# Feed-forward: one matmul of 512 columns for the high weights, with the corrections in a half bank of their own that is added at eviction

## The chip, the cores and the metric

The kernel runs on one core of one Trainium2 chip, in one launch. The metric is the device time of one execution in microseconds (us), the median of several runs.

## The reference

The whole network works on 256 tokens with 1024 features each, in float32. It has two blocks. The first has two layers; each has two feed-forwards and between them a mixer (an RWKV-7 time mix in layer 0, a differential attention with shared keys and values in layer 1). The second block has two attentions side by side with gates (sliding window and stick-breaking), and a PEER layer over 16384 experts. What is computed around the change are the four feed-forwards of the first block:

```python
D_MODEL = 1024; D_FF = 2816; SEQ = 256
def rms_norm(x, g, eps=NORM_EPS):
    xf = x.astype(jnp.float32)
    y = xf * lax.rsqrt(jnp.mean(xf * xf, axis=-1, keepdims=True) + eps)
    return (y * g.astype(jnp.float32)).astype(x.dtype)

def swiglu(h, w_in, w_out):
    gate, up = jnp.split(h @ w_in, 2, axis=-1)
    return (jax.nn.silu(gate) * up) @ w_out
...
for l in range(DEPTH):
    x = x + 0.5 * swiglu(rms_norm(x, ffn_norm[l, 0]), ffn_w_in[l, 0], ffn_w_out[l, 0])
    ...
    x = x + 0.5 * swiglu(rms_norm(x, ffn_norm[l, 1]), ffn_w_in[l, 1], ffn_w_out[l, 1])
```

## The kernel before

**Layout and precision.** Activations are kept transposed: 128 features on the partitions, the 256 tokens as columns, eight such chunks for the 1024 features (`self.x`, tile `xT`). A product in high precision is made from two parts of each operand. A weight tile arrives by DMA (`raw`, 128 x 1024 float32, issued by SyncE, three buffers). `wsplit` makes from it the high part `wh` (ScalarE copies it to float32r, line 255) and the low part `wl` (VectorE subtracts, line 258), four buffers of each. An activation tile (`xs`, or `hh` in the feed-forward) has 512 columns per chunk: the high part in columns 0 to 255, the low part in 256 to 511. `mm3` (line 268) then makes three matmuls of 256 columns into the same half bank of PSUM: `wh` with the high part, `wh` with the low part, `wl` with the high part. `lin` (line 273) does so for a list of chunks. Every matmul of the kernel is recorded at line 243, whatever calls it.

**A feed-forward** (`ffn`, line 402). The 2816 inner features are 22 chunks (`NF`), and for each there is a generator `unit(f)`. It loads two weight tiles (gate and up, eight 128 x 128 weights each), makes 2 x 8 x 3 = 48 matmuls into one PSUM bank of 512 columns (gate in one half, up in the other), and evicts: VectorE multiplies the bank by `rstd`, the reciprocal root of the mean square of each token (line 420, tile `gu`), ScalarE takes Silu of the gate half (line 423), VectorE the product with the up half (line 425, `hv`), and ScalarE and VectorE split it into `hh` (lines 306 and 307). Three units are under way at a time. The scaling of x by the norm's gain has been done ahead, so `rstd` is only needed at eviction; unit 0 computes it.

Then come eight output slices `d`. Each has 22 weights of 128 x 128, in tiles of 8, 8 and 6, and makes 66 matmuls of 256 columns into half a bank. `resid` (line 390) adds half of the sum to x (line 391) and calls `hook`, which prepares the next phase for this chunk: ScalarE scales it by the next norm's gain to the high part of `xs` (line 370, 368 where the low part is not needed), VectorE makes the low part (line 371), ScalarE squares x (line 378) and VectorE adds up the squares (`sqa`, line 379). After the last slice the summed squares go through a small matmul (`smp<-base,sqa`, called the statistics here) to `rstd` (lines 333 and 349).

PSUM banks come from rings by tag: tag mm has two, tag wk four, tag sm two. Units of odd number and odd slices take one of tag mm, the others one of tag wk.

**The stages** in the order of the program, with where they lie in the profile: first feed-forward to about 201 us, RWKV to 482, second feed-forward to 672, third feed-forward to 917, differential attention to 1002, fourth feed-forward to 1190, the second block's attentions to 1365, PEER to the end. The third feed-forward has the projections for the shared keys and values between its units (`extra`); these take banks of tag mm and make their head norms with small matmuls of tag sm.

**What sets the order.** Each engine works its instructions in the order in which they stand; that order comes from the scheduler of the tile framework, which moves instructions of an engine by priority within what their data allow. So the text of the program does not give the order by itself. In the second block the biases of the attention scores are made by ScalarE from a table `btab` (line 733 before, 749 after), which SyncE loads by a DMA (line 840).

Of the kernel before, what the change touches and what calls it, by code (L numbers as in the profile page):

```python
# [9 lines left out]
AF = mybir.ActivationFunctionType  # L10
ALU = mybir.AluOpType
# [3 lines left out]
T = 256  # L15
NF = 22
# [109 lines left out]
def stagger(gens, every, width=99):  # L126
    queue, active, t = list(gens), [], 0
    while queue or active:
        if queue and len(active) < width and (t >= every or not active):
            active.append(queue.pop(0))  # L130
            t = 0
        t += 1
        for g in list(active):
            try:
                next(g)
            except StopIteration:
                active.remove(g)
# [36 lines left out]
class Net:  # L174
# [98 lines left out]
    def lin(self, ps, w, xs, ks, first=True, last=True, j0=0):  # L273
        wh, wl = w
        n = len(ks)
        for j, k in enumerate(ks):
            self.mm3(ps, wh[:, j0 + j], wl[:, j0 + j], xs[:, k], first and j == 0, last and j == n - 1)

    def project(self, src, xs, ps=None):
        w = self.wload(src)  # L280
        p = self.mmt()[:, :T] if ps is None else ps
        self.lin(p, w, xs, range(8))
        return p
# [118 lines left out]
    def ffn(self, n, extra=None, then=None):  # L402
        tc, nc, i = self.tc, self.nc, self.i
        xss, acc = self.begin()
        xs = xss[0]
        with tc.tile_pool(name="ff", bufs=1) as fp:
            hh = fp.tile([128, NF, 512], F32R, name="hh")
            box = {}

            def unit(f):  # L410
                ws = [self.wload(i["ffn_in"][n, f, u]) for u in range(2)]
                yield
                p = self.mmt() if f % 2 else self.wkt("mm")
                for u in range(2):
                    self.lin(p[:, u * T:(u + 1) * T], ws[u], xs, range(8))
                yield
                if f == 0:
                    box["r"] = self.rms(acc)
                t = fp.tile([128, 2, T], F32, name="gu", bufs=2)
                nc.vector.tensor_tensor(t, p.rearrange("p (a b) -> p a b", a=2),  # L420
                                        box["r"][:, None, :].to_broadcast([128, 2, T]), op=ALU.mult)
                s = self.tmp("sg")
                nc.scalar.activation(s, t[:, 0], AF.Silu)
                h = self.tmp("hv")
                nc.vector.tensor_tensor(h, s, t[:, 1], op=ALU.mult)  # L425
                self.split(hh[:, f], h)

            gens = [unit(f) for f in range(NF)]
            if extra:
                more = extra(xss[1], box)  # L430
                gens = gens[:2] + [g for k in range(2, NF) for g in ([gens[k]] + more[k - 2:k - 1])]
            stagger(gens, 1, EVERY["ffn"])
            if then:
                self.pre(then)
            for d in range(8):
                p = (self.mmt() if d % 2 else self.wkt("mm"))[:, :T]
                for k0, k1 in ((0, 8), (8, 16), (16, 22)):
                    w = self.wload(i["ffn_out"][n, d][:, k0:k1], k1 - k0)
                    self.lin(p, w, hh, range(k0, k1), k0 == 0, k1 == NF)
                self.resid(d, p, 0.5)  # L440

    def last_proj(self, src, xs, ready, pin=False):
        early = EVERY["early"]
# [924 lines left out]
```

## Time and profile before

| what | value |
|---|---|
| median of the runs | 2212.38 us |
| runs | 2208.43, 2221.66, 2212.38 us |
| profiled execution, its own time | 2211.49 us |
| its span (first to last instruction) | 2209.7 us |
| granted TensorE clock, mean | 0.994 |
| instructions | 40311 |
| bytes moved by DMA | 351.06 MB, 159 GB/s on the mean |

All durations come from the profiled execution. In the rows below PE is TensorE's matmuls, PEld its weight loads (beside the matmuls), DVE is VectorE, ACT ScalarE, POOL GpSimd, SP SyncE; a q behind a name is the queue that issues its DMAs. "128x256" is partitions by elements. What stands in brackets behind an instruction is how long its engine had stood idle and what ended that. An arrow `a<-b,c` reads "a is written from b and c". A matmul's own duration in a group (281 ns, say) holds its way through the array beside the ones ahead of and behind it; from start to start of matmuls in a row it is less, and that is what a stretch divided by its count gives.

### The profile page before, as it was taken

To read this page: it belongs to the slowest core of one execution; us is meant where nothing else is said; L and a number is where in the kernel's file an instruction comes from. 1 tells how busy PE (TensorE), PEld (TensorE's weight loads), DVE (VectorE), ACT (ScalarE), POOL (GpSimd) and SP (SyncE) were. 2 spreads that over 40 slices of the span, in tenths; PEclk is the share of its full clock that TensorE was granted. 3 is DMA by queue.
4 is the path that set the end of the run, shared out by engine and by line. 5 is a ranking of instruction groups with operands and counts; after the bars stand their busy time and mean duration, and the time that the engine had idled before them with its cause. 6 is when DMAs were issued, how large, how long until landed. Compare 5 with 4: busy or idle time off the path is not lost.

```text
span 2209.7 us, 40311 instructions
## 1 busy us (share of the span) xinstructions
PE 2169.1 (98%) x16048; PEld 2032.6 (92%) x16048; DVE 1533.2 (69%) x2982; ACT 1116.3 (51%) x2070; POOL 78.0 (4%) x109
## 2 busy tenths in 40 slices
PE   8999999989999999999999999999999999999999
PEld 8998777779999999989999999999999999888887
DVE  6665695666666666486666767999489985666665
ACT  5443633344454444475445654444576654554554
POOL 0000040000000000020001000000000000000000
PEclk9999999999999999999999999999999999999999
DMA  6564331135565555435565445555544345555554
GB/s 214 183 180 141 117 105 39 39 105 182 180 183 179 167 179 178 136 112 189 183 180 179 136 145 172 163 172 176 192 138 131 130 145 187 192 192 195 194 192 152
DMA packets 98589, 351.06 MB, mean 159 GB/s; under 512 B 10944, under 2 KB 12480, under 8 KB 98272
## 3 DMA queue, kind: packets, MB, share of 16 engines
q1 hardware_dynamic: 98400, 348.48, 49.2%
q8 instruction: 126, 2.06, 0.4%
q14 instruction: 63, 0.52, 0.1%
HBM read 347.38 MB, written 1.05 MB: 158 GB/s over the span
## 4 chain that ended last, share of the span: by engine, by line
PE 48%; DVE 5%; issue 1%; ACT 0%; DMA 0%; POOLq 0%; POOL 0%; ACTq 0%
PE mm L243 28%; PE y L243 16%; PE pg L243 3%; DVE wl L258 2%; DVE dm L1130 1%; DVE ex L1135 0%; PE sc L243 0%; DVE dm L1133 0%; PE po L243 0%; DVE v L1098 0%; PE tr L762 0%; PE psc L243 0%; DMA raw<-in_p_u_dram 0%; DVE si L1100 0%; PE smp L243 0%
## 5 line engine op out<-in xcount | busy, mean ns | idle before, releaser
L243 PE MATMUL mm<-xs,wh 128*128 128x256 f32 x6304 | 1160.4, 286 | 14.0 <-ACT wh L255 6.8
L243 PEld LDWEIGHTS mm<-xs,wh 128*128 128x128 f32 x6304 | 988.3, 193 | 20.4 <-ACT wh L255 6.8
L258 DVE TENSOR_TENSOR wl<-raw,wh 128x1024 fp32r<-128x1024 f32 (+1 forms) x633 | 765.9, 1210 | 328.0 <-ACT wh L255 327.0
L255 ACT ACTIVATE wh<-raw 128x1024 fp32r<-128x1024 f32 (+1 forms) x633 | 660.5, 1044 | 594.7 <-PE mm L243 472.5
L243 PE MATMUL mm<-xs,wl 128*128 128x256 f32 x3152 | 896.6, 285 | 2.0 <-DVE wl L258 2.0
L243 PEld LDWEIGHTS mm<-xs,wl 128*128 128x128 f32 x3152 | 607.2, 193 | 2.9 <-DVE wl L258 2.9
L243 PE MATMUL y<-wh,cs 128*128 128x512 f32 x1024 | 274.0, 390 | 0.0
L243 PE MATMUL mm<-hh,wh 128*128 128x256 f32 x1408 | 250.1, 281 | 0.0
L243 PEld LDWEIGHTS y<-wh,cs 128*128 128x128 f32 x1024 | 192.3, 188 | 39.6
L243 PEld LDWEIGHTS mm<-hh,wh 128*128 128x128 f32 x1408 | 215.9, 188 | 0.0
L243 PE MATMUL mm<-hh,wl 128*128 128x256 f32 x704 | 198.1, 281 | 0.0
L243 PE MATMUL y<-wl,cs 128*128 128x512 f32 x512 | 157.8, 390 | 0.0
L243 PEld LDWEIGHTS mm<-hh,wl 128*128 128x128 f32 x704 | 132.6, 188 | 0.0
L243 PE MATMUL mm<-xs,raw 128*128 128x256 f32 x512 | 126.1, 394 | 2.5 <-DVE xs L490 2.5
L243 PEld LDWEIGHTS y<-wl,cs 128*128 128x128 f32 x512 | 96.2, 188 | 20.0
L306 ACT ACTIVATE cs<-ga 128x256 fp32r<-128x256 f32 x103 | 43.0, 418 | 136.9 <-PE y L243 136.7
L243 PEld LDWEIGHTS mm<-xs,raw 128*128 128x128 f32 x512 | 96.2, 197 | 16.9 <-DVE xs L490 2.9
L420 DVE TENSOR_TENSOR gu<-mm,rstd 128x512 f32<-128x512 f32 x88 | 60.8, 691 | 44.4 <-PE mm L243 44.2
L306 ACT ACTIVATE hh<-hv 128x256 fp32r<-128x256 f32 x88 | 36.6, 416 | 104.6 <-DVE hv L425 104.6
L307 DVE TENSOR_TENSOR cs<-ga,cs 128x256 fp32r<-128x256 f32 x103 | 43.8, 426 | 55.1 <-ACT cs L306 55.1
L1045 DVE TENSOR_SCALAR ohb<-iota,xT 128x128 f32<-128x128 f32 x192 | 59.5, 343 | 15.3 <-PE pg L243 13.9
L243 PE MATMUL pg<-ohb,xT 128*128 128x128 f32 x512 | 65.9, 276 | 0.0
(320 smaller groups left out, 1883.9 us busy)
## 6 DMA issues: line engine op xcount, KB each, us to landing
raw<-in_ffn_in_dram SPq DMA_DIRECT2D x176, 512.0 KB, 3.8
raw<-in_p_u_dram SPq DMA_DIRECT2D x128, 512.0 KB, 3.7
raw<-in_p_v_dram SPq DMA_DIRECT2D x128, 512.0 KB, 4.3
raw<-in_ffn_out_dram SPq DMA_DIRECT2D x64, 512.0 KB, 3.6
raw<-in_w_in_dram SPq DMA_DIRECT2D x34, 512.0 KB, 3.7
raw<-in_ffn_out_dram SPq DMA_DIRECT2D x32, 384.0 KB, 3.3
raw<-in_w_rkv_dram SPq DMA_DIRECT2D x24, 512.0 KB, 3.7
raw<-in_w_kv_dram SPq DMA_DIRECT2D x16, 512.0 KB, 3.7
```

The lines of the kernel that those rows point to most:

```text
L243: self.nc.tensor.matmul(out, lhsT, rhs, start=start, stop=stop, skip_group_check=True)
L255: hi = nc.scalar.activation(fh[:rows, :w], raw[:rows, :w], AF.Copy)
L258: lo = nc.vector.tensor_tensor(fl[:rows, :w], raw[:rows, :w], fh[:rows, :w].bitcast(F32), op=ALU.subtract)
L306: nc.scalar.activation(dst[rows, :T], src, AF.Copy)
L307: nc.vector.tensor_tensor(dst[rows, T:], src, dst[rows, :T].bitcast(F32), op=ALU.subtract)
L420: nc.vector.tensor_tensor(t, p.rearrange("p (a b) -> p a b", a=2), box["r"][:, None, :].to_broadcast([128, 2, T]), op=ALU.mult)
L1045: nc.vector.tensor_scalar(b, iota, itp[:, 1, t:t + 1], itp[:, 2, t:t + 1], op0=ALU.is_equal, op1=ALU.mult)
L1130: nc.vector.tensor_tensor(m, iota[:, None, :50].to_broadcast([128, 16, 50]), bf[:, h, :, None].to_broadcast([128, 16, 50]), op=ALU.is_equal)
```

## The change

A new `linw` makes, for each chunk, one matmul of 512 columns with `wh` (both parts of the activation at once, into the two halves of a bank) and one of 256 columns with `wl` and the high part, into the second half. The first half then holds high times high, the second both corrections. A new `fold` adds the halves at eviction: ScalarE copies the second half out of PSUM (`low`), VectorE adds the first half to it. A unit now takes two banks, one of tag mm for the gate and one of tag wk for the up half, and two folds; only the gate half is multiplied by `rstd` there. The up half stays unscaled, and so does `hh`; in its place every output slice is multiplied by `rstd` after its fold (tile `fy`), before `resid`. The output slices take a whole bank each. The rest of the program keeps `lin`.

```diff
+    def linw(self, ps, w, xs, ks, first=True, last=True):
+        wh, wl = w
+        n = len(ks)
+        for j, k in enumerate(ks):
+            self.mm(ps, wh[:, j], xs[:, k], first and j == 0, False)
+            self.mm(ps[:, T:], wl[:, j], xs[:, k, :T], False, last and j == n - 1)
+
+    def fold(self, out, p):
+        low = self.tmp("low")
+        self.nc.scalar.activation(low, p[:, T:], AF.Copy)
+        self.nc.vector.tensor_tensor(out, p[:, :T], low, op=ALU.add)
...
-                p = self.mmt() if f % 2 else self.wkt("mm")
-                for u in range(2):
-                    self.lin(p[:, u * T:(u + 1) * T], ws[u], xs, range(8))
+                ps = [self.mmt(), self.wkt("mm")]
+                for p, w in zip(ps, ws):
+                    self.linw(p, w, xs, range(8))
                 yield
                 if f == 0:
                     box["r"] = self.rms(acc)
                 t = fp.tile([128, 2, T], F32, name="gu", bufs=2)
-                nc.vector.tensor_tensor(t, p.rearrange("p (a b) -> p a b", a=2),
-                                        box["r"][:, None, :].to_broadcast([128, 2, T]), op=ALU.mult)
+                for u, p in enumerate(ps):
+                    self.fold(t[:, u], p)
+                nc.vector.tensor_tensor(t[:, 0], t[:, 0], box["r"], op=ALU.mult)
...
-                p = (self.mmt() if d % 2 else self.wkt("mm"))[:, :T]
+                p = self.mmt() if d % 2 else self.wkt("mm")
                 for k0, k1 in ((0, 8), (8, 16), (16, 22)):
                     w = self.wload(i["ffn_out"][n, d][:, k0:k1], k1 - k0)
-                    self.lin(p, w, hh, range(k0, k1), k0 == 0, k1 == NF)
-                self.resid(d, p, 0.5)
+                    self.linw(p, w, hh, range(k0, k1), k0 == 0, k1 == NF)
+                y = self.tmp("fy")
+                self.fold(y, p)
+                nc.vector.tensor_tensor(y, y, box["r"], op=ALU.mult)
+                self.resid(d, y, 0.5)
```

The numbers behind the names below tell tiles apart; the two programs count them differently. Lines of the changed program: fold 288 and 289, multiply of the gate 434, product 438, split of `hv` 319, multiply of an output slice 455, residual 403, scaling 382, square 390, sum of squares 391, `rstd` 361.

VectorE in one unit of the first feed-forward (`gu` the gate and up half, `wl` the low weights of later tiles, `hv` the product), before:

```order
L420 TENSOR_TENSOR gu_773<-mm_712,rstd_210 128x512
L258 TENSOR_TENSOR wl_839<-raw_836,wh_838 128x1024
L425 TENSOR_TENSOR hv_777<-sg_775,gu_773 128x256
L307 TENSOR_TENSOR hh_148<-hv_777,hh_148 128x256
L258 TENSOR_TENSOR wl_902<-raw_899,wh_901 128x1024
```

and in the changed program:

```order
L289 TENSOR_TENSOR gu_566<-mm_520,low_567 128x256
L434 TENSOR_TENSOR gu_566<-gu_566,rstd_195 128x256
L258 TENSOR_TENSOR wl_623<-raw_620,wh_622 128x1024
L289 TENSOR_TENSOR gu_566<-mm_521,low_570 128x256
L438 TENSOR_TENSOR hv_576<-sg_574,gu_566 128x256
L258 TENSOR_TENSOR wl_677<-raw_674,wh_676 128x1024
L319 TENSOR_TENSOR hh_148<-hv_576,hh_148 128x256
```

One instruction on 512 columns became three on 256, and the two splits of weights now stand between the additions and between the product and its split.

ScalarE from the end of the fourth feed-forward into the second block (`xs` the scaling of the last chunk of x, `sq` its square, `bias` made from the table `btab`), before:

```order
L255 ACTIVATE wh_13430<-raw_13428 128x1024
L255 ACTIVATE wh_13475<-raw_13473 128x1024
L370 ACTIVATE xs_12685<-xT_64,vec_65 128x256
L378 ACTIVATE sq_13324<-xT_64 128x256
L255 ACTIVATE wh_13521<-raw_13519 128x1024
L349 ACTIVATE rstd_13328<-smp_13329 128x256
L733 ACTIVATE bias_13423<-btab_13342 128x384
L733 ACTIVATE bias_13425<-btab_13342 128x384
```

and in the changed program:

```order
L255 ACTIVATE wh_12094<-raw_12092 128x1024
L255 ACTIVATE wh_12139<-raw_12137 128x1024
L288 ACTIVATE low_11981<-mm_11917 128x256
L749 ACTIVATE bias_12087<-btab_12006 128x384
L749 ACTIVATE bias_12089<-btab_12006 128x384
L382 ACTIVATE xs_11468<-xT_64,vec_65 128x256
L390 ACTIVATE sq_11988<-xT_64 128x256
L749 ACTIVATE bias_12132<-btab_12006 128x384
L749 ACTIVATE bias_12134<-btab_12006 128x384
L255 ACTIVATE wh_12185<-raw_12183 128x1024
L361 ACTIVATE rstd_11992<-smp_11993 128x256
```

Two biases moved ahead of the scaling and the square of the last chunk, and two more ahead of the next weight split and `rstd`.

VectorE at the end of the first feed-forward (`xT` the residual, `sqa` the sum of squares, `sm` the first step of the statistics, `oka` a constant of the RWKV stage), before:

```order
L391 SCALAR_TENSOR_TENSOR xT_64<-mm_2199,xT_64 128x256
L258 TENSOR_TENSOR wl_2479<-raw_2476,wh_2478 128x1024
L379 TENSOR_TENSOR sqa_1752<-sqa_1752,sq_2285 128x256
L391 SCALAR_TENSOR_TENSOR xT_64<-mm_2288,xT_64 128x256
L476 TENSOR_SCALAR oka_2389<-vec_65 128x8
L379 TENSOR_TENSOR sqa_1752<-sqa_1752,sq_2374 128x256
L333 TENSOR_SCALAR sm_2404<-smp_2401 128x2
```

and in the changed program:

```order
L258 TENSOR_TENSOR wl_2145<-raw_2142,wh_2144 128x1024
L391 TENSOR_TENSOR sqa_1537<-sqa_1537,sq_1968 128x256
L492 TENSOR_SCALAR oka_2055<-vec_65 128x8
L289 TENSOR_TENSOR fy_2034<-mm_1971,low_2035 128x256
L455 TENSOR_TENSOR fy_2034<-fy_2034,rstd_195 128x256
L403 SCALAR_TENSOR_TENSOR xT_64<-fy_2034,xT_64 128x256
L391 TENSOR_TENSOR sqa_1537<-sqa_1537,sq_2040 128x256
L345 TENSOR_SCALAR sm_2070<-smp_2067 128x2
```

Ahead of the last residual there now stand the addition and the multiply of its slice; what follows the residual is as before.

## Rows read from the trace of the kernel before

**Rows 1.** The page: busy time of each engine, and the granted clock in 40 slices.
```profile
PE 2169.1 (98%) x16048; PEld 2032.6 (92%) x16048; DVE 1533.2 (69%) x2982; ACT 1116.3 (51%) x2070; POOL 78.0 (4%) x109
...
PEclk9999999999999999999999999999999999999999
```
**Rows 2.** Chain of waits in order of time, last stretch: start us, us, what.
```profile
1813.61 43.20 PE mm L243 x360
1856.80 348.20 PE y L243 x1536
```
**Rows 3.** Busy times by stretch: a unit, an output slice, units of the third feed-forward.
```profile
core 0: us, PE busy (x) PEld busy (x) DVE busy (x) ACT busy (x) POOL busy (x), PEclk, DMA share, GB/s
63.52:69.28 5.76, 5.76 (x50) 5.76 (x49) 3.90 (x6) 2.73 (x5) 0.00 (x0) 1.00 0.56 186
185.39:193.22 7.83, 7.83 (x68) 7.83 (x67) 4.17 (x5) 3.20 (x4) 0.00 (x0) 1.00 0.62 190
672.00:853.00 181.00, 180.48 (x1495) 178.59 (x1495) 115.51 (x169) 83.17 (x122) 9.61 (x9) 1.00 0.53 173
```
**Rows 4.** Timeline of a unit: start us, us, instruction, idle before it.
```profile
63.44 1.06 ACT L255 ACTIVATE wh<-raw 128x1024 fp32r<-128x1024 f32 x1 [1.70 <-PE mm L243]
63.52 0.69 DVE L420 TENSOR_TENSOR gu<-mm,rstd 128x512 f32<-128x512 f32 x1 [0.52 <-PE mm L243]
```
**Rows 5.** Groups by line, shapes apart: count, busy us, mean ns, idle before.
```profile
L243 PE MATMUL mm<-hh,wl 128*128 128x256 f32 x704 | 198.1, 281 | 0.0
...
L258 DVE TENSOR_TENSOR wl<-raw,wh 128x1024 fp32r<-128x1024 f32 x600 | 734.0, 1224 | 288.3 <-ACT wh L255 287.2
...
L255 ACT ACTIVATE wh<-raw 128x1024 fp32r<-128x1024 f32 x600 | 632.4, 1055 | 545.8 <-PE mm L243 430.0 <-issue 63.8 <-DMA raw<-in_p_u_dram 20.6
...
L420 DVE TENSOR_TENSOR gu<-mm,rstd 128x512 f32<-128x512 f32 x88 | 60.8, 691 | 44.4 <-PE mm L243 44.2
...
L425 DVE TENSOR_TENSOR hv<-sg,gu 128x256 f32<-128x256 f32 x88 | 37.0, 421 | 3.4 <-ACT sg L423 3.4
...
L391 DVE SCALAR_TENSOR_TENSOR xT<-mm,xT 128x256 f32<-128x256 f32 x56 | 23.3, 423 | 25.5 <-PE mm L243 25.3
...
L991 ACT ACTIVATE ga<-mm 128x256 f32<-128x256 f32 x60 | 22.0, 367 | 1.7 <-PE mm L243 1.7
```
**Rows 6.** Timeline of the first feed-forward's end, TensorE and VectorE.
```profile
200.74 0.28 PE L243 MATMUL mm<-hh,wl 128*128 128x256 f32 x1
...
201.05 0.42 DVE L391 SCALAR_TENSOR_TENSOR xT<-mm,xT 128x256 f32<-128x256 f32 x1 [4.17 <-PE mm L243]
...
202.44 0.61 PE L243 MATMUL smp<-base,sqa 128*128 128x1 f32 x4 [1.43 <-DVE sqa L379]
```
**Rows 7.** Timeline of the third feed-forward's end, TensorE and VectorE.
```profile
917.41 2.32 PE L243 MATMUL mm<-xs,raw 128*128 128x256 f32 x10
...
917.61 0.42 DVE L391 SCALAR_TENSOR_TENSOR xT<-mm,xT 128x256 f32<-128x256 f32 x1 [6.01 <-PE mm L243]
...
919.57 0.50 PE L243 MATMUL smp<-base,sqa 128*128 128x1 f32 x4
```
**Rows 8.** Timeline of the fourth feed-forward's end, all engines.
```profile
1190.76 0.33 SPq L840 DMA_DIRECT2D btab<-in_t_b_dram  x1
...
1191.62 0.49 ACT L370 ACTIVATE xs<-xT,vec 128x256 fp32r<-128x256 f32 x1
...
1192.88 0.48 DVE L371 SCALAR_TENSOR_TENSOR xs<-xT,vec,xs 128x256 fp32r<-128x256 f32 x1
...
1193.28 0.42 DVE L379 TENSOR_TENSOR sqa<-sqa,sq 128x256 f32<-128x256 f32 x1
...
1193.76 0.60 PE L243 MATMUL smp<-base,sqa 128*128 128x1 f32 x4
...
1196.20 1.75 ACT L733 ACTIVATE bias<-btab 128x384 f32<-128x384 f32 x4
```
**Rows 9.** View of the tile btab: from its DMA's issue to its landing.
```profile
DMA to landing us min/median/max: 5.4/5.4/5.4
```
**Rows 10.** Busy times by stretch behind the first feed-forward, columns as in rows 3.
```profile
204.00:206.00 2.00, 0.69 (x2) 0.29 (x2) 0.78 (x2) 0.38 (x1) 0.03 (x1) 0.50 0.00 0
```

## The prediction

> **What bounds the kernel now.** I read the page's busy times first [rows 1]: TensorE is busy 98% of the span, VectorE 69%, ScalarE 51%, and the row of granted clocks shows full speed in every slice. Then the chain of waits in order of time, whose last pieces are TensorE alone [rows 2]: 360 matmuls of 256 columns take 43.20 us, 120.0 ns each, and 1536 of 512 columns take 348.20 us, 226.7 ns each. So a matmul costs its columns (106.7 and 213.3 ns at 2.4 GHz) plus 13.3 ns, whichever its width. The reader is to see that two narrow ones cost 240.0 ns and one wide one 226.7.
>
> Then the busy times of one unit and of one output slice [rows 3]. A unit (48 matmuls, 5.76 us, 120.0 ns each) and a slice of the output projection (66 matmuls, 7.83 us, 118.6 ns each) are filled by TensorE; VectorE works 3.90 and 4.17 us in them. The timeline of the unit [rows 4] says who waits for whom: ScalarE waits 1.70 us for TensorE to free a weight buffer, VectorE 0.52 us for the sums. So the feed-forward ends with TensorE, and what TensorE loses there is worth its full time.
>
> **The change part by part.** *Fewer matmuls.* Two matmuls of 256 columns with the same high weights become one of 512. Feed-forward has 4 x 22 x 2 x 8 = 1408 such pairs in the input part and 4 x 8 x 22 = 704 in the output part (the 704 low matmuls of [rows 5] count the latter), so 2112 matmuls go; columns stay the same. Input part: 240.0 - 226.7 = 13.3 ns each, 0.213 us a unit, 18.8 us over 88 units. Output part: 2 x 118.6 = 237.3 ns; a wide one there I take at 213.3 + 12.6, between the two overheads that rows show (12.0 and 13.3), so 11.3 ns each, 7.9 us. Together 26.7 us. The bounds from rows: nothing, if a wide matmul took twice 118.6 to 120 ns here, and 28.2 us, if all 2112 saved 13.3.
>
> Of the rules on this, one speaks against the change. The Trainium skill (TensorE: Matmul & The Clock Gate, Back-to-back issue gap) puts a warm matmul at its columns over 2.4 GHz plus 2.5 ns; by it only 2112 x 2.5 = 5.3 us would go, an estimate. The trace does not agree at either width: 120.0 and 226.7 ns stand where the rule has 109 and 216.
>
> *More work at eviction.* Per unit VectorE loses one 512-column multiply (691 ns) and gets two additions and one multiply of 256 columns; the addition reads PSUM and SBUF as the residual does (423 ns), the multiply is like the 421 ns product [rows 5]. That is +0.57 us: 4.5 us in a unit of 5.55. ScalarE gets two copies out of PSUM, like the 367 ns Gelu that reads it: +0.73 us. In an output slice VectorE gets 0.85 us and ScalarE 0.37. I cost this at nothing while the units run: it lies beside TensorE, in ScalarE's 1.70 us of waiting and in VectorE's 1.86 us without work (5.76 - 3.90). The new order of VectorE puts a weight split between the additions, so nothing stands idle behind the second copy. Four weight buffers let the splits run two half units ahead. In PSUM a unit now takes one bank of each kind; the bank of tag mm comes back two units later, and its addition is done half a unit after the sums. In the third feed-forward the key/value projections share that tag, so a bank alternates between a unit and a projection; VectorE works 115.5 of 181 us there now [rows 3] and gets 22 x 0.57 = 12.5 us more. DMA gets 1 MB per 5.55 us, 189 GB/s, beside the 186 of the unit and 190 of the slice [rows 3].
>
> *The end of each feed-forward.* The last slice is now copied, added, multiplied by rstd and only then added to x: one copy (0.37, with its hand-off 0.41) and two VectorE operations of 0.42, so x is 1.25 us later. What that costs differs at the four ends.
> - Into the RWKV stage [rows 6]: last matmul at 200.74, residual 201.05, statistics matmul 202.44 after 1.43 us of idle TensorE. Nothing covers: +1.25 us.
> - Into the second attention [rows 7]: TensorE runs the ready matmuls of the query projection until the statistics start at 919.57, with no gap. All later steps hang on them: +1.25 us.
> - From the second to the third feed-forward: the new order gives TensorE thirteen pairs of the two halves of the first unit, some 4.7 us, before it needs the last chunk of x, which comes about 4.6 us after the last matmul: a weight split stands in the way (1.06 + 1.22), then copy 0.37, three VectorE operations of 0.42, scaling 0.49 and low part 0.48 in part beside it [rows 5, 8]: 0, and up to 1 us if that is short.
> - Into the second block [rows 8]: here a queue is changed. ScalarE's order now has two biases, made from a table that a DMA brings, ahead of the scaling of the last chunk of x; before, they stood behind rstd. That DMA is issued at 1190.76 (it waits for the memory of hh) and lands 5.4 us later [rows 9], at 1196.2. Behind it come two biases (4 take 1.75 us, 0.44 each), the scaling (ready after 0.49), the low part (0.48) and the square sum (0.42): statistics at about 1198.45, against 1193.76 before. The order puts 17 more matmuls (42 for 25) ahead of them, 2.0 us. So +2.7 us. The ends: 0 if the table is early enough, 4.7 if those matmuls do not help.
>
> I add 0.7 us for what I cannot place: in [rows 10] the granted clock is at half after TensorE idled at the first of these ends (1.2 GHz between 204 and 206), a longer idle at the second block may do the same (bounds 0 and 1.5 us), and the third feed-forward has short waits of TensorE for head norms.
>
> Sum, on the profiled execution's own 2211.5 us (span 2209.7 and 1.8 around it; 0.04% below the median of 2212.4): - 18.8 - 7.9 + 1.25 + 1.25 + 2.7 + 0.7 = - 20.8, so 2190.7, rounded to 2191. That is 1.0% below the median: right on the border of what a measurement of this kernel can tell from no change, 1%.
>
> **The rivals.**
> *The ends cost little.* If the table lands before it is needed and the second attention's wait is filled, of the four ends 2.5 us stay: 2211.5 - 26.7 + 2.5 = 2187.3. For it: TensorE has ready matmuls at three of the four ends. Against it: the table's 5.4 us is a row, and its issue waits for the last matmul. 0.15.
>
> *The overhead is not per matmul here.* If what I call overhead went with the columns moved, a wide matmul would take 2 x 120.0 ns here: nothing saved, and 5.9 us of ends added: 2217. For it: no row has wide and narrow matmuls in turn, nor xs or hh as the moving operand of a wide one. Against it: the 226.7 ns of [rows 2] are measured over 1536 wide ones in a row. 0.08. (With the saving by the rule of the Trainium skill above, 5.3 us, this case would be at 2212.)
>
> *ScalarE and VectorE become the bound of the units (slower).* Each unit is now handed over more often: copy, add, multiply, Silu, product, split, all in order with the weight splits. If VectorE keeps the 1.86 us per unit that it stands idle now and works 4.47 (3.90 + 0.57), a unit takes 6.33 us in place of 5.76: 88 x 0.57 = 50 us lost, with 7.9 gained in the output part and 6 lost at the ends, 2260. It decides from 5.78 us a unit on (no gain left) and is slower by over 1% from 6.03. Against it: part of that idle time is waiting for TensorE itself [rows 4], which shrinks when others get slower, and four weight buffers absorb single delays. 0.11.
>
> **How the numbers follow.** The forecast has 0.66, with its own range 2186 to 2196; about 0.37 of these are more than 1% below 2212.4 (under 2190.3), the rest within 1%. Faster by over 1%: 0.25 of the forecast and 0.14 of the early table, 0.39. Same: 0.41 of the forecast, 0.08 of the second rival and 0.01 of the first, 0.50. Slower: 0.11, of which nearly all over 1%. The range goes from 2184 to 2218: it holds the forecast, the early table and no gain, and leaves out the slower rival and the tails.
>
> **What would show it.** Right: a unit of 5.55 us and an output slice of 7.57 to 7.60 between the same points, wide matmuls some 227 ns apart and the next narrow one 120 behind; 2112 fewer matmuls on the page; TensorE as full as now in the units, VectorE near 4.5 us of them. Behind the first feed-forward the statistics 2.6 to 2.7 us after the last matmul in place of 1.7; at the second block ScalarE's bias with a wait for the table's DMA, and TensorE idle for 2 to 3 us ahead of the statistics. Wrong: units of 5.7 us with a full TensorE (the overhead stayed), matmuls that wait for wh, wl or a copy within the units (the others became the bound), or no wait at the second block.

## The result and the profile after

| | median, us | runs | ratio to before, 95% interval |
|---|---|---|---|
| before, beside it | 2214.22 | 5 | |
| changed | 2198.59 (2197.19 to 2203.62) | 5 | 0.994 [0.9928, 0.9952] |
| before, with the next set of runs | 2210.14 | 17 | |
| changed, once more | 2197.40 (2195.70 to 2199.57) | 6 | 0.9941 [0.9927, 0.9954] |

So 0.6% faster, 13 to 16 us, where 21 us were forecast: within the range and within 1%. The profiled execution (2203.62 us, span 2201.8) is the longest of the five. In the RWKV stage TensorE had 0.59 of its clock between 446 and 467 us, and 0.84 there before:

```profile
446.00:467.00 21.00, 15.43 (x67) 12.15 (x67) 9.27 (x25) 4.92 (x10) 2.15 (x2) 0.59 0.00 1
```
```profile
446.00:467.00 21.00, 15.46 (x95) 12.18 (x96) 11.91 (x35) 5.16 (x11) 2.15 (x2) 0.84 0.00 1
```

Whether the change has a part in that is not shown: the same program has 0.67 there in run 1 below, and run 3, which ends its feed-forwards as before, has 0.66. So the stages are compared one by one, and the total of this trace comes at the end.

The page after, busy times and granted clock, answers to [rows 1]:

```profile
PE 2156.8 (98%) x13936; PEld 1927.3 (88%) x13936; DVE 1594.9 (72%) x3222; ACT 1171.6 (53%) x2278; POOL 79.5 (4%) x109
...
PEclk9999999989999999999999999999999999999999
```

The 2112 matmuls are gone (16048 to 13936), and TensorE is as full as before. Busy times by stretch (columns as in [rows 3]) first for one unit and one output slice, then for long stretches of two input parts and two output parts:

```profile
62.23:67.89 5.66, 5.66 (x34) 4.89 (x33) 4.31 (x9) 3.27 (x6) 0.00 (x0) 1.00 0.59 185
182.21:189.92 7.71, 7.71 (x47) 6.75 (x46) 4.93 (x7) 3.55 (x5) 0.00 (x0) 1.00 0.61 195
...
40.00:120.00 80.00, 80.00 (x455) 69.34 (x454) 60.78 (x100) 46.80 (x86) 0.00 (x0) 1.00 0.58 187
1010.00:1110.00 100.00, 100.00 (x579) 88.23 (x578) 77.54 (x127) 58.88 (x108) 0.00 (x0) 1.00 0.58 190
...
140.00:190.00 50.00, 50.00 (x287) 43.85 (x286) 31.63 (x44) 22.25 (x32) 0.00 (x0) 1.00 0.62 192
852.00:902.00 50.00, 50.00 (x290) 43.99 (x289) 31.71 (x47) 25.88 (x39) 0.00 (x0) 1.00 0.64 186
```

A unit went from 5.76 to 5.66 us, not to 5.55; a slice from 7.83 to 7.71, not to 7.60. The long stretches show why. A count has about two matmuls that reach in over the border; without them the first input part gives 80.00/453 = 176.6 ns a matmul, **353 ns for a pair of wide and narrow**, and the fourth, by the same instructions with the same full TensorE and clock, 100.00/577 = 173.3, **347 ns a pair**. The forecast was 226.7 + 120.0 = 346.7. The output parts differ too: 351 ns a pair in the first feed-forward, 347 in the third. There are two paces, where the rows of before had shown only narrow ones at 120.0 and at 118.6 ns.

Groups by line, shapes apart, for the eviction ([rows 5] has what they replace):

```profile
L255 ACT ACTIVATE wh<-raw 128x1024 fp32r<-128x1024 f32 x600 | 633.6, 1056 | 577.2 <-PE mm L243 294.3 <-issue 232.2 <-DMA raw<-in_p_u_dram 18.4
...
L288 ACT ACTIVATE low<-mm 128x256 f32<-128x256 f32 x208 | 75.9, 365 | 16.3 <-PE mm L243 16.3
L289 DVE TENSOR_TENSOR gu<-mm,low 128x256 f32<-128x256 f32 x176 | 73.3, 418 | 0.5 <-ACT low L288 0.5
...
L434 DVE TENSOR_TENSOR gu<-gu,rstd 128x256 f32<-128x256 f32 x88 | 37.4, 425 | 3.6 <-ACT rstd L361 0.8
```

Copy 365 ns, addition 418, multiply 425: the forecast took 367, 423 and 421. VectorE works 4.31 us in a unit, 4.5 were forecast.

The end of the first feed-forward in the timeline answers to [rows 6]:

```profile
197.51 0.28 PE L243 MATMUL mm<-hh,wl 128*128 128x256 f32 x1
...
197.83 0.38 ACT L288 ACTIVATE low<-mm 128x256 f32<-128x256 f32 x1 [5.50 <-PE mm L243]
...
198.25 0.42 DVE L289 TENSOR_TENSOR fy<-mm,low 128x256 f32<-128x256 f32 x1 [0.24 <-ACT low L288]
198.70 0.42 DVE L455 TENSOR_TENSOR fy<-fy,rstd 128x256 f32<-128x256 f32 x1
199.16 0.42 DVE L403 SCALAR_TENSOR_TENSOR xT<-fy,xT 128x256 f32<-128x256 f32 x1
...
200.55 1.01 PE L243 MATMUL smp<-base,sqa 128*128 128x1 f32 x4 [2.76 <-DVE sqa L391]
```

Copy, addition, multiply and residual stand in a row, and the statistics come 3.04 us after the last matmul in place of 1.70: 1.34 more, 1.25 forecast. TensorE idles 2.76 us instead of 1.43, and the granted clock behind that is lower. Twelve microseconds from just ahead of the statistics, before and after:

```profile
202.00:214.00 12.00, 8.07 (x30) 6.45 (x31) 9.32 (x26) 0.38 (x1) 0.70 (x1) 0.72 0.11 27
```
```profile
200.00:212.00 12.00, 7.92 (x24) 6.33 (x25) 8.85 (x25) 0.42 (x2) 0.70 (x1) 0.57 0.01 4
```

The granted clock is 0.57 on the mean, 0.72 before: more of the stretch is spent at 1.2 GHz, the lower of the two levels. Into the second attention (against [rows 7]) the statistics come 3.44 us after the last matmul, 2.27 before:

```profile
910.56 0.28 PE L243 MATMUL mm<-hh,wl 128*128 128x256 f32 x1
...
914.00 0.61 PE L243 MATMUL smp<-base,sqa 128*128 128x1 f32 x4
```

And the end of the fourth feed-forward, to hold against [rows 8] and [rows 9]:

```profile
1180.25 0.33 SPq L856 DMA_DIRECT2D btab<-in_t_b_dram  x1
...
1183.08 0.94 ACT L749 ACTIVATE bias<-btab 128x384 f32<-128x384 f32 x2 [1.61 <-DMA btab<-in_t_b_dram]
...
1185.46 0.50 PE L243 MATMUL smp<-base,sqa 128*128 128x1 f32 x4
...
1187.06 0.43 PE L357 MATMUL smp<-base,sm 128*128 128x128 f32 x2 [0.51 <-POOL sm L348]
...
1188.42 0.39 PE L243 MATMUL mm<-xs,wh 128*128 128x256 f32 x1 [0.69 <-DVE pj L868]
```

ScalarE does wait for the table (1.61 us), as the order said. But the table lands 2.8 us after its issue, not 5.4 as before, and TensorE has matmuls until the statistics (one wait, of 0.16 us). What idles comes behind them (0.51 and 0.69 us), since `rstd` is late.

### The profile page after: what moved, and what is told of

Same layout as the page of the kernel before. It is cut to its first block, busy times and chain, and to the rows that moved or that the text cites. A ratio compares the mean times of both kernels' runs of the same rounds, so it can differ in the third digit from the quotient of the medians.

```text
span 2201.8 us, 36597 instructions
## 1 busy us (share of the span) xinstructions
PE 2156.8 (98%) x13936; PEld 1927.3 (88%) x13936; DVE 1594.9 (72%) x3222; ACT 1171.6 (53%) x2278; POOL 79.5 (4%) x109
## 4 chain that ended last, share of the span: by engine, by line
PE 48%; DVE 5%; issue 1%; ACT 0%; DMA 0%; POOLq 0%; POOL 0%; ACTq 0%
PE mm L243 28%; PE y L243 16%; PE pg L243 3%; DVE wl L258 2%; DVE dm L1146 0%; PE sc L243 0%; DVE ex L1151 0%; DVE dm L1149 0%; PE po L243 0%; DVE v L1114 0%; PE tr L778 0%; PE psc L243 0%; ACT wh L255 0%; DVE si L1116 0%; DMA raw<-in_p_u_dram 0%
## 5 line engine op out<-in xcount | busy, mean ns | idle before, releaser
L243 PE MATMUL mm<-xs,wh 128*128 128x256 f32 (+1 forms) x4896 | 1149.4, 319 | 17.0 <-ACT wh L255 6.9
L243 PEld LDWEIGHTS mm<-xs,wh 128*128 128x128 f32 x4896 | 814.7, 192 | 84.1 <-ACT wh L255 6.9
L243 PE MATMUL mm<-hh,wh 128*128 128x512 f32 x704 | 246.5, 393 | 0.0
L243 PEld LDWEIGHTS mm<-hh,wh 128*128 128x128 f32 x704 | 132.2, 188 | 30.2
L288 ACT ACTIVATE low<-mm 128x256 f32<-128x256 f32 x208 | 75.9, 365 | 16.3 <-PE mm L243 16.3
L289 DVE TENSOR_TENSOR gu<-mm,low 128x256 f32<-128x256 f32 x176 | 73.3, 418 | 0.5 <-ACT low L288 0.5
```

What stands on the lines that cost most here:

```text
L243: self.nc.tensor.matmul(out, lhsT, rhs, start=start, stop=stop, skip_group_check=True)
L288: self.nc.scalar.activation(low, p[:, T:], AF.Copy)
L289: self.nc.vector.tensor_tensor(out, p[:, :T], low, op=ALU.add)
```

## The experiments

Two questions: what sets the pace of a pair, and what the ends cost. All medians stand beside 2210 to 2211 for the kernel before.

**1. The changed kernel again** (nothing edited).

> The changed kernel once more, nothing edited. In the trace after the change a pair of a wide and a narrow matmul takes either 346.7 ns from start to start (all of the second and fourth feed-forward's input parts, 226.7 + 120.0 as predicted) or 351 to 354 ns (the first one's input part, half of the third's, most output parts). Theory A (the pace is fixed by the program, by what lies where): the same stretches show the same pace again, and the median is again 2197 to 2201 us. Theory B (the pace is left over from a chance disturbance ahead): other stretches are slow now, 7 ns x 352 pairs = 2.5 us an input part, and single runs spread by several us.

2197.40 us, in the table above. The same two stretches and the second feed-forward's:

```profile
40.00:120.00 80.00, 80.00 (x464) 70.53 (x463) 62.28 (x101) 47.41 (x87) 0.00 (x0) 1.00 0.59 193
490.00:590.00 100.00, 100.00 (x568) 86.70 (x567) 76.52 (x125) 57.67 (x107) 0.00 (x0) 1.00 0.55 184
1010.00:1110.00 100.00, 100.00 (x578) 88.16 (x578) 77.66 (x127) 58.88 (x108) 0.00 (x0) 1.00 0.59 189
```

The first input part is now at the fast pace (80.00/462 = 173.2, 346 ns a pair), the second at the slow one (353 ns), which it was not in the first trace (100 us held 576 there). One program, two executions, other stretches: theory B for the input parts. The output parts have the same pace in both (x286 and x291 in the stretches shown above, x287 and x290 there).

**2. Wide ones together, narrow ones together.**

```diff
         for j, k in enumerate(ks):
             self.mm(ps, wh[:, j], xs[:, k], first and j == 0, False)
+        for j, k in enumerate(ks):
             self.mm(ps[:, T:], wl[:, j], xs[:, k, :T], False, last and j == n - 1)
```

> The same matmuls, but for each weight tile all wide ones first and then all narrow ones, in place of pairs in turn. Theory A (turn by turn is what costs: a pair in turn can fall into a slower pace): every pair takes 226.7 + 120.0 = 346.7 ns or less, first input part 2.5 us shorter than after the change, output parts 0.8 us each, third input part about 1.5: 6 to 7 us less than the changed kernel, about 2192 us. Rival (the overhead is only half saved because it goes with the data, or with the operands' places): no change against the changed kernel, 2198 us, and pairs of 351 to 354 in the same stretches.

2196.36 us, 0.994 [0.9922, 0.9958]: no change against the changed kernel. The first feed-forward's stretch:

```profile
40.00:120.00 80.00, 80.00 (x458) 70.28 (x458) 61.93 (x101) 46.87 (x87) 0.00 (x0) 1.00 0.59 192
```

80.00/456 = 175.4, some 350 ns for a wide and a narrow one (in groups of eight the stretch need not hold as many of both), between the two paces. Turn by turn is not what costs; theory A falls. The third output part lost the faster pace here (x285 in 852 to 902 us, x290 with the change).

**3 and 4. One part alone.** Input part: the unit as changed, with `rstd` on both halves, and the output loop of before. Output part: the unit of before, and wide output slices with copy and addition.

```diff
-                    self.linw(p, w, hh, range(k0, k1), k0 == 0, k1 == NF)
-                y = self.tmp("fy")
-                self.fold(y, p)
-                nc.vector.tensor_tensor(y, y, box["r"], op=ALU.mult)
-                self.resid(d, y, 0.5)
+                    self.lin(p, w, hh, range(k0, k1), k0 == 0, k1 == NF)
+                self.resid(d, p, 0.5)
```

```diff
-                ps = [self.mmt(), self.wkt("mm")]
-                for p, w in zip(ps, ws):
-                    self.linw(p, w, xs, range(8))
+                p = self.mmt() if f % 2 else self.wkt("mm")
+                for u in range(2):
+                    self.lin(p[:, u * T:(u + 1) * T], ws[u], xs, range(8))
...
                 self.fold(y, p)
-                nc.vector.tensor_tensor(y, y, box["r"], op=ALU.mult)
                 self.resid(d, y, 0.5)
```

> The wide matmuls in the input part alone; the output part is that of the kernel before, one half bank, no copy and no addition, and rstd is multiplied into both halves of the unit again (one VectorE multiply of 512 columns in SBUF, longer than the 256-column one by 0.2 to 0.4 us a unit). By my steps the input part has 12 to 15 us of the gain in the changed kernel's trace and the ends lose nothing here: 2199 to 2202 from 2214. If VectorE sets the pace of the units (rival), slower than the changed kernel by several us.

2196.51 us, 0.9939 [0.9923, 0.9954]. From the first matmul to the first output matmul it took 126.70 us, 131.38 before and 128.90 in the first trace of the change: the first input part was at the fast pace here.

> The wide matmuls in the output part alone, with copy and addition ahead of the residual but no multiply by rstd there (the units are those of the kernel before). By the changed kernel's trace each output part saves 0.9 us, 3.6 in all, and each end is late by a copy and an addition, 0.8 us, at three ends: about 1 us of gain, 2213, not to be told from before. If the output part's saving were the 7.9 us that I predicted: 2209.

2211.20 us, 1.0001 [0.9991, 1.0012]. The input part alone has the whole gain (run 3). The output part gives 0.9 us each time (62.54 to 61.66 from its first to its last matmul) and loses it at the ends.

**5. The last slice as before.** `rstd` goes back into both halves in the units; slices 0 to 6 are wide, slice 7 narrow.

```diff
-                    self.linw(p, w, hh, range(k0, k1), k0 == 0, k1 == NF)
+                    (self.lin if d == 7 else self.linw)(p, w, hh, range(k0, k1), k0 == 0, k1 == NF)
```

> All wide as in the change, but the last output slice of each feed-forward is the narrow one of before (no copy, no addition), and rstd is multiplied into both halves in the units, not into the output slices. Theory (the ends cost what the copy, the addition and the multiply put ahead of the last residual): the statistics come 1.7 and 2.3 us after the last matmul again behind the first and third feed-forward (3.04 and 3.44 with the change), and the output part keeps 7/8 of its 0.88 us: 62.54 - 0.77 = 61.8. With 352 pairs an input part at 7 to 13 ns each the median is 2193 to 2196 us beside 2210. Rival (the end is covered anyway, it is the clock that costs): as the changed kernel, 2197.

2191.53 us, 0.9908 [0.9892, 0.9923]: about 6 us better than the changed kernel, more than forecast. The statistics come 1.71 and 2.27 us after the last matmul again, and the clock behind the first end is back to 0.72:

```profile
197.00:209.00 12.00, 8.11 (x30) 6.53 (x31) 9.32 (x26) 0.38 (x1) 0.70 (x1) 0.72 0.09 28
```

From that end's last matmul to the first output matmul of the second feed-forward it took 403.55 us, against 409.01 in run 1. Of the 5.46 some 2.3 are the pace of the second input part (352 pairs at 346 in place of 353), 1.33 the end itself; the remaining 1.8 go with a higher clock, here and between 446 and 467 us (0.84, and 0.67 in run 1). The pace and that later clock differ between executions without such an edit too, so the trace bears out the ends, and not the whole 6 us.

**6 and 7. The place of the moving operand.** What sets the output parts apart is where hh starts: behind 16 KB of shared keys and values and one small tile in the third feed-forward, 16416 bytes further on. So tiles were moved by 32 bytes in each partition, with a tile of 8 floats ahead of them.

```diff
+            if n != 2:
+                pad = fp.tile([128, 8], F32, name="pad")
+                nc.gpsimd.memset(pad[:, :1], 0.0)
             hh = fp.tile([128, NF, 512], F32R, name="hh")
```

> As the run with the narrow last slice, and hh of the first, second and fourth feed-forward starts 32 bytes further in each partition (a tile of 8 floats ahead of it), so that it starts at a multiple of 64 bytes as it does in the third, behind the shared keys and values. In the traces so far an output pair takes 351.7 ns in the first, second and fourth feed-forward and 346.8 in the third, in every run. Theory A (the place of the moving operand sets that pace): 346 to 347 in all four, 0.8 us less at three output parts, 2.4 us in all. Theory B (it is something else in the third feed-forward, such as its other transfers): no change, 351.7 in the three.

2189.82 us, 0.990 [0.9884, 0.9916]. Stretches of 45 us in the first, second and third output part:

```profile
138.00:183.00 45.00, 45.00 (x261) 39.65 (x260) 27.06 (x36) 20.81 (x31) 0.00 (x0) 1.00 0.62 191
612.00:657.00 45.00, 45.00 (x261) 39.61 (x261) 30.83 (x46) 25.91 (x42) 0.00 (x0) 1.00 0.64 193
850.00:895.00 45.00, 45.00 (x261) 39.66 (x260) 26.62 (x37) 23.57 (x36) 0.00 (x0) 1.00 0.62 187
```

261 in each, and 250 in 43 us of the fourth: 347 ns a pair in all of them. Theory A. (The third had no new pad and is as before.) The median does not tell this run from run 5. Then the xs tiles:

```diff
         self.xp = pool("acts", bufs=1)
+        pad = self.xp.tile([128, 8], F32, name="pad")
+        nc.gpsimd.memset(pad[:, :1], 0.0)
```

> As the run with the narrow last slice, and both xs tiles start 32 bytes further, at a multiple of 64; everything behind them moves along, so hh is at a multiple of 64 in the first, second and fourth feed-forward and 32 bytes over one in the third. Theory A (place of the moving operand): output pairs 346.7 in the first, second and fourth, 351.7 in the third, the other way round than before; and the input part has one pace, 346.7, in all feed-forwards, in place of one of two by chance. Theory B (not the place): 351.7 in the first, second and fourth and 346.8 in the third as ever, and input parts at either pace.

2188.75 us, 0.9898 [0.9882, 0.9914]. Third and fourth output part, and PEER's wide matmuls:

```profile
842.00:885.00 43.00, 43.00 (x246) 37.31 (x245) 24.84 (x33) 21.47 (x33) 0.00 (x0) 1.00 0.62 189
1112.00:1155.00 43.00, 43.00 (x250) 37.85 (x249) 27.38 (x39) 22.14 (x34) 0.00 (x0) 1.00 0.63 190
...
1900.00:2100.00 200.00, 200.00 (x858) 161.01 (x858) 118.11 (x144) 97.81 (x143) 0.00 (x0) 1.00 0.57 188
```

The other way round, as forecast: the third output part is now the slow one (352 ns), and all four input parts hold 347 ns (three of the four did in run 5 too). The median does not tell this run from runs 5 and 6. But PEER lost: 200 us hold 858 wide matmuls there, 233 ns each, and 884 before (226.7 ns):

```profile
1900.00:2100.00 200.00, 200.00 (x884) 165.73 (x883) 121.23 (x148) 100.96 (x148) 0.00 (x0) 1.00 0.59 193
```

**8. Every copy and addition twice.**

```diff
         self.nc.scalar.activation(low, p[:, T:], AF.Copy)
+        self.nc.scalar.activation(low, p[:, T:], AF.Copy)
+        self.nc.vector.tensor_tensor(out, p[:, :T], low, op=ALU.add)
```

> The changed kernel with every copy and every addition of the eviction made twice, which changes nothing in the result: 0.73 us more of ScalarE and 0.84 of VectorE in each unit, 0.37 and 0.42 in an output slice. My step (the eviction lies beside TensorE in the units): only the ends lose, 0.8 us at three of them, so 2199 to 2201 beside 2197. Rival (the units are bound by VectorE, 4.5 us of 5.6 now and 5.3 then, with splits of weights late behind it): each of 88 units longer by up to 0.84 us, 2220 and more.

2197.55 us, 0.9933 [0.9915, 0.9952]: nothing that could be told. In the first input part

```profile
40.00:120.00 80.00, 80.00 (x464) 70.53 (x463) 72.08 (x132) 57.15 (x116) 0.00 (x0) 1.00 0.57 192
```

VectorE works 72.08 us of 80 (60.78 with the change), and TensorE still holds the fast pace. The statistics are 0.87 and 1.25 us later at the first and third end (3.91 and 4.69), some 2 us that the spread of the runs (2193.74 to 2199.70) covers. The cover in the units is real.

**9 to 12. Which distance.** Three pads (xs; hh of the third feed-forward; `cs`, PEER's stationary operand), on the kernel of run 5 (run 9) and on the kernel before (run 11); and one pad ahead of everything from the raw weights on, with the one of hh (run 10).

```diff
+            if n == 2:
+                pad = fp.tile([128, 8], F32, name="pad")
+                nc.gpsimd.memset(pad[:, :1], 0.0)
             hh = fp.tile([128, NF, 512], F32R, name="hh")
...
+        pad = gp.tile([128, 8], F32, name="pad")
+        nc.gpsimd.memset(pad[:, :1], 0.0)
         def v_unit(j, last):
...
         self.mhalf = self.cp.tile([128, 4], F32, name="mhalf")
+        pad = self.cp.tile([128, 8], F32, name="pad")
+        nc.gpsimd.memset(pad[:, :1], 0.0)
```

> The padded xs of the run before, hh at a multiple of 64 bytes in all four feed-forwards, and a third pad ahead of cs in PEER, so that cs is again 32 bytes over a multiple of 64, as in the kernel before. In the run with padded xs the wide matmuls of PEER (cs the stationary operand, the weights moving) took 233.3 ns in place of 226.7, since cs had moved along, while narrow ones of xs took 117 in place of 120. Theory (place of the operands): pairs 346.8 ns in all input and output parts, PEER's narrow ones 117, its wide ones 226.7 again: 1536 x 6.6 = 10 us and one output part's 1.1 us less than the run with padded xs, 2177 to 2179. Rival (PEER's 233.3 came from something else): 2187 to 2189.

2187.49 us, 0.9891 [0.9877, 0.9905]. Forecast 2177 to 2179: the rival holds, PEER's wide ones stay at 233, and the third output part is slow (x245 in 43 us).

> The narrow last slice, and everything from the raw weights on starts 32 bytes further: moving operand and stationary weights (wh, wl) both at a multiple of 64 bytes, in PEER too. Theory A (the place of the one relative to the other counts): like both at 32 over, so narrow matmuls of xs 120 ns, wide ones of PEER 226.7, pairs at 346.8 or 353 by chance, about 2191. Theory B (each place by itself, the moving operand at a multiple of 64 being good): narrow 117, pairs 346.8, and PEER's wide ones 233 or less.

2193.73 us, 0.9922 [0.9904, 0.9939].

```profile
40.00:120.00 80.00, 80.00 (x464) 70.53 (x463) 65.32 (x104) 48.63 (x89) 0.00 (x0) 1.00 0.60 191
490.00:590.00 100.00, 100.00 (x568) 86.67 (x567) 79.18 (x125) 58.96 (x107) 0.00 (x0) 1.00 0.57 185
...
1900.00:2100.00 200.00, 200.00 (x884) 165.65 (x883) 121.58 (x147) 100.19 (x147) 0.00 (x0) 1.00 0.60 194
```

With activations and weights moved together the input parts and PEER are as unmoved: two paces, and 884 wide ones. The third output part, whose hh has a pad of its own here, is slow (x257 in 850 to 895 us, x262 with the change). Theory A: not the place of one tile counts but its distance from the other.

> The kernel before, without the wide matmuls, with the three pads of the first run of this set (xs and hh at a multiple of 64 bytes, cs 32 over). Theory (place of the operands): three narrow matmuls take 351 to 353 ns in place of 360 in the input parts and 352 in place of 355.5 in the output parts, PEER's input products 117 in place of 120: 1408 x 8 = 11 us, 3 x 176 x 3.5 = 2, 3072 x 3 = 9, and some in the other projections: about 2186 from 2210. That would put a pair's gain from the wide matmul at about 5 ns with either operand place. Rival: 2210, as before.

2199.52 us, 0.9953 [0.9936, 0.9971]: with no wide matmul, pads alone gave the kernel before 11 us, most of what the change gives, though PEER's wide ones cost it 10 us again (x859); the 2186 expected had left that cost out. The first input part, padded and, for comparison, of before:

```profile
40.00:120.00 80.00, 80.00 (x688) 80.00 (x687) 55.92 (x72) 39.56 (x58) 0.00 (x0) 1.00 0.57 188
```
```profile
40.00:120.00 80.00, 80.00 (x669) 80.00 (x668) 54.07 (x70) 38.26 (x56) 0.00 (x0) 1.00 0.57 184
```

Narrow ones at 80.00/686 = 116.6 ns in place of 120.0. So the 13.3 ns that I called a fixed cost of a matmul is partly the place of its operands. And with the operands so placed, three narrow ones take 350 ns and a pair 347 (run 9): there the wide matmul saves 3 ns and not 13. Runs 9 and 11, both with all pads, have spans of 2188.0 and 2195.4 us: 7.4 us apart, with the ends as before in both. In the output parts the theory held for two of the three that it was to speed up: 43 us of the fourth hold 369 (363 before), 45 us of the second 386 (382), but the first has 381 in both.

The last run set the distance, moving minus stationary operand in the built program modulo 128 bytes, to 32 in all eight parts of the feed-forwards and to 0 in PEER:

```diff
             if n == 2:
-                pad = fp.tile([128, 8], F32, name="pad")
+                pad = fp.tile([128, 24], F32, name="pad")
...
-        pad = gp.tile([128, 8], F32, name="pad")
+        pad = gp.tile([128, 24], F32, name="pad")
```

> The runs so far, sorted by how far the moving operand starts from the stationary one, modulo 128 bytes (read off the built programs): 0 in the input parts of before and change (two paces, 346.8 and 352.8 ns a pair; narrow alone 120.0; wide alone in PEER 226.7), 32 in the runs with padded xs and in every output part at 346.8 (narrow alone 117), 64 and 96 wherever an output pair took 353 and PEER's wide ones 233.3. Here xs and hh stand at 32 in all feed-forwards (hh of the third moved on by 96 bytes) and cs at 0 (pad of 96 bytes ahead of it). Theory (that distance sets the pace): pairs 346.8 in all eight parts, PEER's narrow ones 117 and its wide ones 226.7: 1536 x 6.6 = 10 us and 1.1 us less than the 2187.5 of the run with three pads of 32 bytes, 2176 to 2178. Rival (the distance only happens to fit): PEER's wide ones again 233, 2187.

2188.20 us, 0.9902 [0.9885, 0.992].

```profile
842.00:885.00 43.00, 43.00 (x250) 38.12 (x250) 26.18 (x36) 22.44 (x35) 0.00 (x0) 1.00 0.63 188
...
1900.00:2100.00 200.00, 200.00 (x862) 162.13 (x862) 118.11 (x145) 98.51 (x144) 0.00 (x0) 1.00 0.56 188
```

All eight parts are at 347 ns, the third output part too. PEER is not back: 862 where 884 were wanted.

| distance modulo 128 bytes | where | a pair |
|---|---|---|
| 0 | input parts of the change and of runs 1, 5, 6, 10 | 346 or 353, by chance |
| 0 | output parts 1, 2, 4 of the change and of run 1 | about 351 |
| 32 | output part 3 of the change; all of runs 6, 7 and 12 that were set so | 347 |
| 64, 96 | output part 3 of runs 7 and 10, and of run 9 | 352 to 354 |

What stays open: why PEER's wide matmuls, alone in a row, do not follow it. They ran at 226.7 wherever nothing in their operands was moved against the other, and at 232 to 233 with distances of 96 (run 7), 64 (runs 9 and 11) and 0 modulo 128 (run 12). Read modulo 256 off the same built programs the rows no longer clash: the input parts, and PEER where it ran at 226.7, stand at 0; the output parts 1, 2 and 4 of the change, and PEER in run 12, at 128; the pairs at 347 at 32 or 160; those at 352 to 354 at 192 and 224. That is a fit made afterwards: no run put PEER back to 0 modulo 256 behind moved activations. And two rows do not follow it: the first output part of run 11, and the third of run 2, both at 160, both slow. Why there are two paces at distance 0 was not found either.

## Why the prediction was right and wrong

- **The class and the range** held: 0.6%, within 1%, the likeliest of the three. But 2197 to 2199 us lie above the forecast's own 2186 to 2196: the steps below make some 5 to 8 us less than the 20.8, and the wide range covered it. Of the signs, a unit took 5.66 us in the first trace, close to the 5.7 that was to show the prediction wrong, and 5.54 at the faster pace (32 x 173.2); the slice came to 7.71, not 7.57 to 7.60.
- **Fewer matmuls, input part** (18.8 us forecast): the step "13.3 ns each" gives the right size at the fast pace (360.0 to 347 ns, for three narrow ones and for a pair) and twice too much at the slow one (353, 7 ns). Its reason, a fixed 13.3 ns whichever the width, does not hold: run 11 takes 3.4 of them off a narrow one by the operands' place alone, and 3 ns a pair are left to save there. That it was right at the place where xs stands is in part luck. In the first trace the four parts gave some 2.5, 4.6, 3.5 and 4.6 us, 15.2 together. The 3.5 is the stretch from the second feed-forward's last matmul to the third's first output matmul, 183.16 to 179.64; the others are 352 pairs at their pace.
- **Fewer matmuls, output part** (7.9 us): this term was the most mis-sized. I took 213.3 + 12.6 ns for the wide one; 61.66 us over 176 pairs is 350.3 a pair, against 62.54/176 = 355.3, so 5.0 ns were saved where 11.3 were forecast, 3.6 us in all four. The narrow ones were at 118.6 there and not at 120.0, which goes at least in part with the place of hh (run 11), and I took that difference for noise. Both parts: 18.8 of 26.7 us in the first trace, 18.7 in run 1. The rival that the overhead goes with the columns is wrong in the input part of the change, more than half true in the output part, and mostly true in the input parts with the pads.
- The Trainium skill (TensorE: Matmul & The Clock Gate, Back-to-back issue gap) would have put the gain at 2.5 ns a pair, an estimate from its figure. Between the change and the kernel before the runs show 5.0 to 13, and with the pads in both 3; and they show no stretch of 256-column matmuls below 116 ns where it has 109: neither its figure nor mine.
- **The eviction beside TensorE**: right, with all three durations within 2%; run 8 shows that twice the work is hidden too. That rival is out.
- **The ends**: 1.34 us (1.25 forecast) at the RWKV stage, 1.17 (3.44 from last matmul to statistics, 2.27 before) at the second attention, nothing from second to third feed-forward, as forecast. The sign "2.6 to 2.7 us after the last matmul in place of 1.7" mixes two counts: 1.70 is from that matmul's start, where 1.25 more makes 2.95 (3.04 measured), and 2.68 is the idle time, 1.43 + 1.25 (2.76 measured). At the second block the sum was right by luck and its mechanism wrong: the forecast said TensorE would idle 2 to 3 us ahead of the statistics for a table that lands after 5.4 us. It landed after 2.8, TensorE did not idle there, and waited behind the statistics. From the last output matmul to the statistics behind the block's attentions it took 179.83 us in the first trace and 178.33 in run 1, 177.05 before: 2.8 and 1.3 us lost, 2.7 forecast. In the narrow-last-slice run 5 it was 177.02.
- **The 0.7 us for the clock** was in the right place: 0.57 of the clock for 12 us behind the first end in place of 0.72; from the statistics to the first projection it took 5.23 us in place of 4.78, of which the four matmuls of the statistics have 0.40 (1.01 us, 0.61 before). Run 5, with the end of before, has 0.72 again. What the clock took later in the RWKV stage is not in this term.

Sum by these, in the first trace: - 15.2 - 3.6 + 1.34 + 1.17 + 2.8 + 0.45 = - 13.0. That trace's span is only 7.9 us shorter (2201.8 for 2209.7). Some 4.7 of the missing 5 lie between the first feed-forward's last matmul and the second's first output matmul: 410.84 us, 409.02 before, where pace and end account for 2.9 less; the RWKV stage, with the low clock of above, lies there. In run 1, for which - 15.1 - 3.6 + 1.34 + 1.17 + 1.3 + 0.45 = - 14.4, the span is 14.9 us shorter (2194.8). The medians are 13 to 16 us apart. So the term that was mis-sized is that of the matmuls: 18.8 us in place of 26.7. The ends cost 5.8 us in the first trace and 4.3 in run 1, where 5.9 were forecast.

## What to carry to other kernels

Fewer, wider matmuls save the gap between them, but count the gap for the operands that will stand there: a pace from one tile (120.0 and 226.7 ns here) need not hold for another, and some of that gap can be had without any wide matmul. Where one row differs by 1.5 ns from its like, ask why before calling it noise; here tiles of 8 floats gave the kernel before nearly as much as the whole change. And do not pay for such a gain at the last slice before a dependence: run 5 kept seven slices wide, left the eighth as it was, and came to 0.9908 [0.9892, 0.9923] where the change had 0.9941 [0.9927, 0.9954].

## What was not expected of the hardware

- The pace of a stream of matmuls changed when one operand's tile was moved by 32 bytes against the other's (runs 6, 7, 11), and not when both were moved (run 10): 116.6 or 120.0 ns at 256 columns, 226.7 or 233 at 512, 346 to 354 for the two in turn. Which distances are good was not settled for all rows.
- At one distance the same program runs a whole input part at 346 ns a pair in one execution and at 353 in the next.
- 1.33 us more of idle TensorE at one place took the granted clock of the next 12 us from 0.72 to 0.57; without them it was 0.72 again (run 5).
